# A tenth pair of up-projection tiles by half-size products in a fused decoder layer

## The chip, the cores and the metric

The kernel is one program on one core of a Trainium2 chip. The metric is device microseconds (us) of one execution. "The time before" is the median of three runs of the kernel as it stood.

## The reference, cut to what matters

One decoder layer, all in 32-bit floats, 512 tokens, model width 1024: a mixing sub-layer (not touched here) and then a gated MLP. `u` has 2 x 2816 columns: 22 column blocks of 128 in each of two halves, the half that goes through the silu and the half that it multiplies.

```python
h2 = rmsnorm(x, norm2_g[l]) * (1.0 + sc2) + sh2          # (512, 1024)
u = causal_dwconv(h2 @ w_up[l], conv_w[l], conv_b[l])    # w_up: (1024, 5632); conv over 3 tokens
a, v = jnp.split(u, 2, axis=-1)
x = x + gt2 * ((jax.nn.silu(a) * v) @ w_down[l])         # w_down: (2816, 1024)
```

## The kernel before

**Numbers in two parts.** TensorE takes its operands in a reduced format, so every operand is kept as a high part (a rounded copy, made on ScalarE) and a low part (what the rounding lost, made on VectorE as source minus high part). This pair of parts is called a form here. One product is three matmuls: high by high, low by high, high by low (`mm3`, L156 to L158). A second way to make a low part is used for some forms ("added"): ScalarE writes the negated source into the low part, GpSimd issues a DMA that adds the source to it, and the rounding of the format leaves the loss; VectorE then has nothing to do.

**The up-projection.** The result is made transposed, in 44 tiles of 128 columns of `u` by 512 tokens, each in a PSUM bank. Tile `2f` is block `f` of the silu half, tile `2f+1` the same block of the other half. A standard tile is 8 products (the 1024 inputs in eighths) of a 128x128 weight block with all 512 tokens, so 24 matmuls of 512 columns. Nine pairs of tiles (8 and 9, 12 and 13, ..., 40 and 41) are made together by seven half-size products in the manner of Strassen and Winograd, each of them 4 blocks by 256 tokens, so 12 matmuls of 256 columns: `P1` to `P7`. They need sums and differences of the quarters of the weights (`quads`: two tiles by two halves of the inputs), which VectorE makes in place in the loaded weights, and of the quarters of `h2` (`hB`, made into forms 1 to 4 of `h2`, `hS`, once for all pairs). The names in the order of steps:

- `n1` takes the loaded weights of the pair and makes weight form 1; `ns`, `nc`, `na`, `s4` make a sum of quarters (`e`) and three differences (in `raw`); `n5` is form 5; `f6 f2 f7 f3 f4` are the other five forms (tiles `wq`, 128x512).
- `P1` and `P5` come first, into bank `u` of the odd tile and into a spare bank `ux`. `S` is a ScalarE copy of the result of `P1` into the bank of the even tile; `P6` is then added to the result of `P1`, so `P6` waits for `S`. `w` is a ScalarE copy of `P5` to `w5u`. `V` and `W` (VectorE) add that copy to what `u` holds after `P6` and after `P7`, so `P7` waits for `V` and `P4` for `W`.
- `m0`, `m1` make the forms of the next two standard tiles (`whi`, `wlo`); `B0 B1 C0 C1` are the products of those tiles, in two pieces each, placed between the half-size products.
- `q6` or `p0` is the work on a finished tile 6 or 0 of a unit (`up_post`): ScalarE scales it with a tap of the convolution (L1646), VectorE adds the other two taps (L1647, L1648), ScalarE applies silu to an even tile (L1651), VectorE multiplies the pair (L1654). `x` takes one step from a list of further work on finished pairs (`gP`, `gQ`, `s`, `st`: operands for the down-projection), `g` and `G` steps of another gate, `t` steps that form the quarters of `h2`.

**What sets the order.** It is written by hand in two strings. `PRO` is played once: tiles 0 to 7 and the preparation of the first pair. `UNIT` is then played nine times, for pairs `j` = 2 to 10; in it a primed step belongs to the next pair. Every engine plays its instructions in the order of these strings, and waits by semaphores for what the others must have done. In the trace's times `PRO` covers tile 3 from 344.76 us, tile 4 from 350.23, tile 5 from 355.67, tiles 6 and 7 after it; the first `P1` of `UNIT` starts at 372.44. Loaded weights (`raw`) sit in three buffers that are filled from SyncE's queue as they come free.

Of the kernel before, what the change touches and what calls it, by code (L numbers as in the profile page):

```python
# [15 lines left out]
AF = mybir.ActivationFunctionType  # L16
ALU = mybir.AluOpType
# [7 lines left out]
KT = D // P  # L25
# [15 lines left out]
NB = 2  # L41
NU = 10
AWAY = (0, 1, 2, 3, 4, 5)
CUT = {"B": 6, "C": 7}
ADD = (1, 1)
PLAIN = ""
PRO = ("t t x M1 M2 t t t t F3 M3 F4 t A5 q0 G M4 q1 q2 F6 q3 M5 G M6 A7 x q4 x q5 G x t x n1' ns' f2' nc' n5' q6 na' s4' m0' x x M7 m1' g x f6' f7' x x x x f4'")
UNIT = ("P1 S P5 w n1' ns' x f3 B0 P6 P2 B1 V x f2' nc' n5' h1 x p-1 f4' P7 x m0' P3 h0' W K p2 g na' p0 C0 P4 x x x C1 s4' p1 x m1' x f6' x x x f7'")
PREP = ('sq2 sq3 rq2 rq3', '', 'nq0', 'fq0', 'nq1', '', 'lq0', 'fq1', 'nq2', '', 'lq1', 'fq2', 'nq3', 'lq2', 'fq3',
        'lq3', 'sk0 rk0 sk1 rk1', 'nk0 fk0 sk2 rk2', 'nk1 fk1 sk3 rk3', 'lk0 nk2 fk2', 'lk1 nk3 fk3 sa0 ra0',  # L50
# [61 lines left out]
def hybrid_layer_kernel(ctx: ExitStack, tc: tile.TileContext, d: dict, out: bass.AP, dbg=None):  # L112
    nc = tc.nc
    ve, sc, gp, pe, sp = nc.vector, nc.scalar, nc.gpsimd, nc.tensor, nc.sync
# [12 lines left out]
    def nm(s):  # L127
        uid[0] += 1
        return f"{s}_{uid[0]}"

    def G(shape, dt=F32, s="g"):
        return gran.tile([P] + list(shape), dt, tag="g", name=nm(s))

    def PS(s="ps"):
        return psum.tile([P, 512], F32, tag="b", name=nm(s))
# [12 lines left out]
    def f32(ap):  # L148
        return ap.bitcast(F32)

    def split(hi, lo, src, eng=None):
        sc.copy(hi, src)  # L152
        (eng or ve).tensor_tensor(lo, src, f32(hi), ALU.subtract)  # L153

    def mm3(o, ah, al, bh, bl, start, stop):
        pe.matmul(o, ah, bh, start=start, stop=False, skip_group_check=True)  # L156
        pe.matmul(o, ah, bl, start=False, stop=False, skip_group_check=True)  # L157
        pe.matmul(o, al, bh, start=False, stop=stop, skip_group_check=True)  # L158
# [56 lines left out]
    def issue():  # L215
        if len(issued) < len(loads):
            name, shape, pieces = loads[len(issued)]
            if name[0] == "d" and shape[0] * shape[1] <= 1024:
                raw = G(shape, s="rawd")
            else:  # L220
                raw = wp.tile([P] + shape, F32, tag="raw", name=nm("raw"), bufs=3)
            for sl, src in pieces:
                sp.dma_start(raw[sl], src)
            issued.append(raw)
# [3 lines left out]
    def take(name):  # L228

        i = taken[0]  # L230
        assert loads[i][0] == name, (loads[i][0], name)
        while len(issued) < min(i + (5 if loads[min(len(issued), len(loads) - 1)][0][0:2] in ("dx", "dy") else 3), len(loads)):
            issue()
        taken[0] += 1
        return issued[i]
# [55 lines left out]
    def next_parts(more=True, g=False, added=False):  # L291
        if not ahead:
            piece(g)
        w = ahead.pop(0)
        if more:
            piece(added=added)
        return w
# [1135 lines left out]
    def gate_step(n=2):  # L1433
        for _ in range(n):
            next(ada2, None)
# [105 lines left out]
    hB = {}  # L1541
# [83 lines left out]
    us = {}  # L1625
# [3 lines left out]
    def up_mm(st, sl, ks=range(KT)):  # L1629
        if st not in us:  # L1630
            us[st] = PS("u")
            if st not in wts:
                wts[st] = next_parts(st < nst - 2, added=False)
        hi, lo = wts[st]
        for k in ks:
            mm3(us[st][:, sl], hi[:, k], lo[:, k], h2T[k // 2][0][:, k % 2, sl], h2T[k // 2][1][:, k % 2, sl],
                k == 0 and not sl.start, k == KT - 1)
# [20 lines left out]
    quads = {}  # L1658
    forms7 = {}
    held = {}  # L1660
# [4 lines left out]

    def h2_form(o, q):
        hS[q] = hi, lo = [G([4, 256], F32R, s="hS") for _ in range(2)]
        split(hi, lo, hB.pop(o))

    tw = [(h2_sum, (0, 0), (0, 1), (0, 0)), (h2_sum, (0, 1), (1, 1), (0, 1)), (h2_sum, (1, 1), (1, 1), (0, 0)),  # L1670
          (h2_form, (0, 0), 1), (h2_sum, (1, 0), (1, 0), (1, 1)), (h2_form, (1, 1), 2), (h2_form, (0, 1), 3),
# [7 lines left out]
    def half_form(src):  # L1679
        t = G([2, 4, P], F32R, s="wq")  # L1680
        split(t[:, 0], t[:, 1], src)
        return t[:, 0], t[:, 1]

    def pair_open(j):
        raw = take(f"up{2 * j}")
        quads[j] = [raw[:, s, 4 * h:4 * h + 4] for s in range(2) for h in range(2)]
        t = wp.tile([P, 2, KT, P], F32R, tag="aw", name=nm("w3"), bufs=1)
        forms7[j] = {n: (t[:, 0, h:h + 4], t[:, 1, h:h + 4]) for n, h in ((1, 0), (5, 4))}
        split(*forms7[j][1], quads[j][0])
# [13 lines left out]
    def std_form(src, added):  # L1703
        hi = wp.tile(list(src.shape), F32R, tag="whi", name=nm("whi"))
        lo = wp.tile(list(src.shape), F32R, tag="wlo", name=nm("wlo"))
        if added:
            sc.activation(lo, src, AF.Copy, scale=-1.0)  # L1707
            gp.dma_start(f32(lo), src, accum_op=ALU.add)  # L1708
            return (hi, lo), lambda: sc.copy(hi, src)
        split(hi, lo, src)  # L1710
        return (hi, lo), None
# [13 lines left out]
    def std_make(j, s):  # L1725
        st = 4 * j + 2 + s
        if s == 0:
            raws[j] = take(f"up{2 * j + 1}")
        wts[st], high[st] = std_form(raws[j][:, s], ADD[s] and (s or j > NB))

# [5 lines left out]
        sc.copy(ws5[j], us["x", j][:, lo_half])  # L1736

    def banks(j):
        us[4 * j + 1] = PS("u")
        us["x", j] = PS("ux")  # L1740
        us[4 * j] = (held.pop if j == NU else held.get)(0)

    ws5 = {}

    def u_of(j, n, sl):
        return us[4 * j + n][:, sl]

    def do(j, tok):
        last = j == NU
# [8 lines left out]
    def do_(j, tok):  # L1758
        last = j == NU
        lo_, hi_ = lo_half, hi_half  # L1760
        w = forms7.get(j)
        u = partial(u_of, j)
        if tok == "P1":
            banks(j)
            sprod(u(1, lo_), w[1], h2_quarter(0, lo_), True)
            if last:
                pe.matmul(u(1, hi_), w[1][0][:, 0], h2_quarter(0, lo_)[0][0], start=False, stop=False,
                          skip_group_check=True)
        elif tok == "P5":
            sprod(us["x", j][:, lo_], w[5], h2_summed(1), True)  # L1770
        elif tok == "P6":
            sprod(u(1, lo_), w[6], h2_summed(2))
        elif tok == "P2":
            sprod(u(0, lo_), w[2], h2_quarter(1, lo_))
        elif tok == "P7":
            sprod(u(1, lo_), w[7], h2_summed(3))
        elif tok == "P3":
            sprod(u(0, hi_), w[3], h2_quarter(1, hi_))
        elif tok == "P4":
            sprod(u(1, lo_), w[4], h2_summed(4))  # L1780
        elif tok in ("B0", "B1", "C0", "C1"):
            up_mm(4 * j + (2 if tok[0] == "B" else 3), full, (range(0, CUT[tok[0]]), range(CUT[tok[0]], KT))[int(tok[1])])
        elif tok == "S":
            sc.copy(u(0, lo_), u(1, lo_))
        elif tok == "w":
            spare(j)
        elif tok == "V":
            ve.tensor_tensor(u(0, hi_), u(1, lo_), ws5[j], ALU.add)
        elif tok == "W":
            ve.tensor_tensor(u(1, hi_), u(1, lo_), ws5[j], ALU.add)  # L1790
        elif tok[0] == "p":
            up_post(4 * j + int(tok[1:]))
        elif tok == "x":
            step(1)
        elif tok in ("g", "G"):
            gate_step(2 if tok == "g" else 1)
        elif tok == "t":
            turn()
        elif tok[0] == "m":
            std_make(j, int(tok[1]))  # L1800
        elif tok[0] == "h":
            h = high.pop(4 * j + 2 + int(tok[1]))
            if h:
                h()
        elif tok == "K":
            park_late()
        elif tok == "n1":
            pair_open(j)
        elif tok == "ns":
            pair_sum(j)  # L1810
        elif tok == "nc":
            pair_less(j, 2, 0, 2)
        elif tok == "na":
            pair_less(j, 0, 4, 0)
        elif tok == "s4":
            pair_less(j, 1, 1, 0)
        elif tok == "n5":
            split(*w[5], quads[j][4])
        else:
            pair_form(j, int(tok[1]), {6: 0, 2: 1, 7: 2, 3: 1, 4: 3}[int(tok[1])])  # L1820
# [45 lines left out]
    def park_late():  # L1866
        if late26:
            j, st34 = late26.pop(0)
            sc.dma_start(pk34[:, j], f32(st34))
            gp.dma_start(pk26[:, AWAY.index(j)], f32(gQ.pop(j)))  # L1870
# [104 lines left out]
    lo_half, hi_half, full = slice(0, 256), slice(256, 512), slice(0, 512)  # L1975
# [27 lines left out]
    made[0] = 1  # L2003
    for tok in PRO.split():
        if tok[0] == "M":
            up_mm(int(tok[1]), full if tok[1] > "2" else hi_half)
            if tok == "M2":
                held[0] = us[0]
        elif tok[0] in "FA":
            piece(added=tok[0] == "A")  # L2010
            wts[int(tok[1])] = ahead.pop(0)
        elif tok[0] == "q":
            up_post(int(tok[1]))
        elif tok[0] in "txgG":
            do_(1, tok)
        else:
            do(NB - 1, tok)
# [71 lines left out]
    for q in range(NQ):  # L2089
        w = ready.pop(0)  # L2090
# [38 lines left out]
```

## Time and profile before

| | |
|---|---|
| median of 3 runs (671.79 to 672.07) | 671.82 us |
| the profiled execution: its time, and its span in the trace | 672.72 us, 670.9 us |
| PE (TensorE matmuls) busy | 663.2 us, 99% of the span |
| DVE (VectorE) busy | 582.8 us, 87% |
| ACT (ScalarE) busy | 400.5 us, 60% |
| POOL (GpSimd) busy | 74.1 us, 11% |

The profiled execution is 0.90 us above the median of the runs, 0.13%. Its span leaves out 1.8 us around the program. In a row of the trace's timeline stand: start, duration, engine, line, operation, tile written and tiles read, shape, and in brackets the idle time of the engine ahead of it and who ended that. Matmuls are pipelined: each starts before the one ahead has ended, so the pace is read from the starts.

### The profile page before, as it was taken

Reading aid. Unit: us, or ns where it says so; the run is one execution under the profiler, and the core shown is the slowest. Engines: PE = TensorE matmul, PEld = TensorE weight load, DVE = VectorE, ACT = ScalarE, POOL = GpSimd, SP = SyncE. Lnnn points to the kernel's source line nnn. Section 1 sums busy time; section 2 is a strip of 40 time slices with the busy share of each in tenths; the row PEclk is TensorE's granted clock in tenths of the full one; section 3 lists DMA queues with packets and bytes.
Section 4 is the critical chain, followed back from the end, with each engine's and each line's share of the span. In section 5 each row is a group of like instructions: output and inputs, shape, how many; then the busy total and the mean of one; then the engine's idle time right before and its main releaser. Section 6 shows DMA issues by size and latency. Waiting matters only on the chain.

```text
span 670.9 us, 11080 instructions
## 1 busy us (share of the span) xinstructions
PE 663.2 (99%) x4072; PEld 567.9 (85%) x4072; DVE 582.8 (87%) x1173; ACT 400.5 (60%) x775; POOL 74.1 (11%) x100
## 2 busy tenths in 40 slices
PE   8999999999999999999999999999999999999997
PEld 4677898788898889888998989999899998888886
DVE  4688988999998997789988999888988888988787
ACT  5565446766677688334665776577765775553431
POOL 1006144200100000211100111010110110000000
PEclk9999999999999999999999999999999999999999
DMA  9999443398042132537436488877889759999932
GB/s 278 286 321 271 149 157 130 100 293 264 26 149 95 33 103 96 195 103 220 153 95 157 103 228 240 239 214 211 228 236 250 224 153 345 366 343 398 380 111 95
DMA packets 111880, 134.84 MB, mean 201 GB/s; under 512 B 7322, under 2 KB 84946, under 8 KB 111826
## 3 DMA queue, kind: packets, MB, share of 16 engines
q1 hardware_dynamic: 102961, 106.89, 50.2%
q0 software_dynamic: 4720, 16.26, 10.7%
q10 hardware_dynamic: 4144, 10.99, 4.3%
q8 instruction: 32, 0.52, 0.3%
q14 instruction: 23, 0.18, 0.1%
HBM read 107.11 MB, written 16.00 MB: 183 GB/s over the span
## 4 chain that ended last, share of the span: by engine, by line
PE 91%; SPq 3%; DMA 2%; DVE 2%; issue 1%; ACT 0%; ACTq 0%; DVEq 0%
PE u L157 11%; PE u L156 11%; PE u L158 11%; PE dn L157 5%; PE dn L156 5%; PE dn L158 5%; PE pT L156 3%; PE pT L158 3%; PE pT L157 3%; PE F L1063 3%; PE oT L1091 3%; PE oh L158 2%; PE oh L156 2%; PE oh L157 2%; PE lev L1192 2%; SPq L321 2%
## 5 line engine op out<-in xcount | busy, mean ns | idle before, releaser
L156 PE MATMUL u<-h2h,whi 128*128 128x512 f32 (+1 forms) x200 | 75.1, 375 | 0.0
L157 PE MATMUL u<-h2l,whi 128*128 128x512 f32 (+1 forms) x200 | 74.9, 374 | 0.0
L158 PE MATMUL u<-h2h,wlo 128*128 128x512 f32 (+1 forms) x200 | 74.5, 373 | 0.0
L158 PEld LDWEIGHTS u<-h2h,wlo 128*128 128x128 f32 x200 | 37.7, 189 | 6.8
L1031 ACT ACTIVATE pt<-pt,mx 128x128 f32<-128x128 f32 (+3 forms) x64 | 35.8, 562 | 12.1 <-DVE mx L1015 11.1
L156 PEld LDWEIGHTS u<-h2h,whi 128*128 128x128 f32 x200 | 37.9, 189 | 5.5
L157 PEld LDWEIGHTS u<-h2l,whi 128*128 128x128 f32 x200 | 37.9, 189 | 5.2
L156 PE MATMUL pT<-hT,whi 128*128 128x512 f32 x96 | 39.2, 409 | 0.0
L153 DVE TENSOR_TENSOR wlo<-raw,whi 128x1024 fp32r<-128x1024 f32 (+1 forms) x31 | 36.0, 1161 | 3.6 <-ACT whi L152 3.4
L1651 ACT ACTIVATE y<-y 128x512 f32<-128x512 f32 x22 | 13.9, 633 | 41.7 <-DVE y L1648 41.6
L158 PE MATMUL pT<-hT,wlo 128*128 128x512 f32 x96 | 37.7, 393 | 0.0
L157 PE MATMUL pT<-hT,whi 128*128 128x512 f32 x96 | 37.6, 392 | 0.0
L152 ACT CAST whi<-raw 128x1024 fp32r<-128x1024 f32 (+1 forms) x31 | 30.9, 998 | 10.4 <-PE kva L158 4.4
L1647 DVE SCALAR_TENSOR_TENSOR y<-u,cv,y 128x511 f32<-128x511 f32 x44 | 32.8, 745 | 5.0 <-ACT y L1646 5.0
L1070 ACT COPY pT<-F 128x512 f32<-128x512 f32 (+2 forms) x52 | 25.8, 502 | 15.4 <-PE F L1063 11.2
L1015 DVE CUSTOM_DVE_ANT_0 pt<-S,cmask 128x128 f32<-128x128 f32 (+3 forms) x64 | 29.7, 485 | 5.7 <-PE S L1010 5.6
L1648 DVE SCALAR_TENSOR_TENSOR y<-u,cv,y 128x510 f32<-128x510 f32 x44 | 32.9, 749 | 1.5
L397 POOL TENSOR_TENSOR hrs<-hrs,mhalf 128x4 f32<-128x4 f32 (+2 forms) x16 | 20.9, 1314 | 120.7 <-DVE hrs L396 120.6
L1646 ACT ACTIVATE y<-u,cv 128x512 f32<-128x512 f32 x44 | 33.8, 770 | 0.0
L1708 POOL DMA_DIRECT2D wlo<-raw x17 | 14.6, 859 | 166.2 <-ACT wlo L1707 74.6
L153 DVE TENSOR_TENSOR wq<-raw,wq 128x512 fp32r<-128x512 f32 x45 | 30.7, 685 | 0.5 <-ACT wq L152 0.5
L158 PE MATMUL u<-hS,wq 128*128 128x256 f32 x108 | 30.6, 284 | 0.0
(471 smaller groups left out, 2175.3 us busy)
## 6 DMA issues: line engine op xcount, KB each, us to landing
raw<-in_w_up SPq DMA_DIRECT2D x44, 512.0 KB, 5.7
aw<-in_w_ada SPq DMA_DIRECT2D x24, 512.0 KB, 3.8
raw<-in_w_down SPq DMA_DIRECT2D x10, 1024.0 KB, 5.4
wlo<-raw POOLq DMA_DIRECT2D x19, 512.0 KB, 5.2
ada<-in_w_ada SPq DMA_DIRECT2D x32, 256.0 KB, 5.9
raw<-in_w_in SPq DMA_DIRECT2D x7, 1024.0 KB, 6.0
rawd<-in_w_down SPq DMA_DIRECT2D x12, 512.0 KB, 10.5
pk<-st ACTq DMA_DIRECT2D x11, 512.0 KB, 6.5
```

Of the source, the lines that this page charges most:

```text
L152: sc.copy(hi, src)
L153: (eng or ve).tensor_tensor(lo, src, f32(hi), ALU.subtract)
L156: pe.matmul(o, ah, bh, start=start, stop=False, skip_group_check=True)
L157: pe.matmul(o, ah, bl, start=False, stop=False, skip_group_check=True)
L158: pe.matmul(o, al, bh, start=False, stop=stop, skip_group_check=True)
L397: gp.tensor_tensor(o, o, mhalf[:, 0:n], ALU.pow)
L1015: ve.tensor_tensor_reduce(pt[:, sl], ps[:, sl], cmask[:, 512 - W:512], -1.0, 1e30, ALU.add, ALU.min, mx[:, e:e + 1])
L1031: sc.activation(pt[:, sl], pt[:, sl], AF.Exp, bias=mx[:, e:e + 1], scale=-1.0, accum_out=su[:, h % 2, e:e + 1])
L1070: sc.copy(pT, ps[:, 0:n * P])
L1646: sc.activation(y, u, AF.Identity, bias=cv[:, 132 + c:133 + c], scale=cv[:, 88 + c:89 + c])
L1647: ve.scalar_tensor_tensor(y[:, 1:], u[:, :T - 1], cv[:, 44 + c:45 + c], y[:, 1:], ALU.mult, ALU.add)
L1648: ve.scalar_tensor_tensor(y[:, 2:], u[:, :T - 2], cv[:, c:c + 1], y[:, 2:], ALU.mult, ALU.add)
```

## The change

Tiles 6 and 7 are no longer made by 48 matmuls of 512 columns at the end of `PRO`, but as a tenth pair by 84 matmuls of 256 columns (pair 1, `base(1)` = 6), which stand between tile 4 and the first `UNIT`, with tile 5 cut in two pieces (`Y0`, `Y1`) between them. The forms and differences of that pair are made in `PRO`. The low part of form 4 of `h2` is made the added way (`FADD`), in place of the low part of tile 7's weights; the weights of tile 6 and 7 are no longer made into standard forms.

```diff
+FADD = (4,)
-PRO = ("t t x M1 M2 t t t t F3 M3 F4 t A5 q0 G M4 q1 q2 F6 q3 M5 G M6 A7 x q4 x q5 G x t x n1' ns' f2' nc' n5' q6 na' s4' m0' x x M7 m1' g x f6' f7' x x x x f4'")
+PRO = ("t t x M1 M2 t t t t F3 M3 F4 t A5 q0 no G ns nc M4 n1 q1 n5 t na f6 x f2 P1 S P5 w q2 s4 G x P6 P2 Y0 V x f7 q3 x P7 f3 f4 n1' G q4 P3 W Y1 q6 ns' nc' P4 n5' m0' x f2' na' q5 f6' x s4' x m1' x g x f7' x x x f4'")
...
     def h2_form(o, q):
         hS[q] = hi, lo = [G([4, 256], F32R, s="hS") for _ in range(2)]
-        split(hi, lo, hB.pop(o))
+        src = hB.pop(o)
+        if q in FADD:
+            sc.activation(lo, src, AF.Copy, scale=-1.0)
+            gp.dma_start(f32(lo), src, accum_op=ALU.add)
+            sc.copy(hi, src)
+        else:
+            split(hi, lo, src)
...
+    def base(j):
+        return 4 * j if j >= NB else 4 * NB - 2
...
     def banks(j):
-        us[4 * j + 1] = PS("u")
+        us[base(j) + 1] = PS("u")
         us["x", j] = PS("ux")
-        us[4 * j] = (held.pop if j == NU else held.get)(0)
+        us[base(j)] = (held.pop if j == NU else held.get)(0)
...
+        elif tok[0] == "Y":
+            up_mm(5, full, (range(0, 5), range(5, KT))[int(tok[1])])
```

Where it moves instructions, three places. **ScalarE around the new pair's `w`.** Before, what follows tile 1's scaling (`y<-u_3919`, the row ahead of the first one shown) is tile 2's scaling and silu, and then the forms of tiles 6 and 7 from `raw_3853`:

```order
L1646 ACTIVATE y_4161<-u_3970,cv 128x512
L1651 ACTIVATE y_4161<-y_4161 128x512
L152 CAST w_795_4169<-raw_3853 128x1024
L1646 ACTIVATE y_4172<-u_4082,cv 128x512
L263 ACTIVATE wlo_4234<-raw_3853 128x1024
L265 CAST whi_4233<-raw_3853 128x1024
L152 CAST gP_4159<-y_4123 128x256
L1646 ACTIVATE y_4240<-u_4129,cv 128x512
```

Now `S` and `w` of the new pair stand there, then tile 2's scaling and silu, form 7 (`wq_4266`), tile 3's scaling, forms 3 and 4, the next pair's form 1 (`w_814`), tile 4's scaling (`u_4135`) and silu, and tile 6's scaling (`u_3894`, the held bank):

```order
L1798 COPY u_3894<-u_4186 128x256
L1750 COPY w5u_4213<-ux_4187 128x256
L1647 ACTIVATE y_4215<-u_3970,cv 128x512
L1652 ACTIVATE y_4215<-y_4215 128x512
L153 CAST wq_4266<-raw_3853 128x512
L1647 ACTIVATE y_4269<-u_4082,cv 128x512
L153 CAST wq_4290<-raw_3853 128x512
L153 CAST wq_4293<-raw_3853 128x512
L153 CAST w_814_4299<-raw_4107 128x512
L1431 COPY gt_3318<-ps_4221 128x512
L1647 ACTIVATE y_4303<-u_4135,cv 128x512
L1652 ACTIVATE y_4303<-y_4303 128x512
```

Tile 2's scaling moved behind a copy that needs the result of `P5`, and the work on tiles 3, 4 and 6 moved behind it.

**ScalarE ahead of the first `UNIT`'s `S`** (the copy of `u_4340` before, of `u_4399` now). Before, with tile 6's silu and the high part of the first standard tile (`whi`) at the head:

```order
L1651 ACTIVATE y_4274<-y_4274 128x512
L152 CAST whi_4284<-raw_4166 128x1024
L152 CAST gQ_4177<-y_4161 128x256
L1707 ACTIVATE wlo_4317<-raw_4166 128x1024
L152 CAST st_798_4178<-y_4161 128x256
L152 CAST wq_4325<-raw_4107 128x512
L152 CAST wq_4328<-raw_4107 128x512
L152 CAST gP_4159<-s_792_4160 128x256
L152 CAST gQ_4177<-s_792_4160 128x256
L152 CAST st_799_4179<-s_792_4160 128x512
L152 CAST wq_4337<-raw_4107 128x512
L1784 COPY u_3894<-u_4340 128x256
```

Now, from tile 5's scaling on (ahead of these rows stand tile 6's silu, `w_814<-e` for form 5, `whi_4355` and form 2, `wq_4360`):

```order
L1647 ACTIVATE y_4364<-u_4249,cv 128x512
L153 CAST wq_4371<-raw_4107 128x512
L153 CAST gQ_4274<-y_4215 128x256
L1721 ACTIVATE wlo_4379<-raw_4128 128x1024
L153 CAST st_809_4275<-y_4215 128x256
L153 CAST gP_4168<-s_795_4169 128x256
L153 CAST wq_4389<-raw_4107 128x512
L153 CAST gQ_4274<-s_795_4169 128x256
L153 CAST st_810_4276<-s_795_4169 128x512
L153 CAST wq_4396<-raw_4107 128x512
L1798 COPY u_3894<-u_4399 128x256
```

The nine instructions right ahead of `S` are the same as before in number and kinds; form 6 (`wq_4371`) is now the first of them, and form 5, form 2 and tile 5's scaling came in between tile 6's silu and them.

**VectorE in the same place.** Before, with the low parts of form 5 (`w_812<-e`), tile 6's two taps, two differences, and the low part of the first standard tile:

```order
L153 TENSOR_TENSOR w_812_4263<-e_4266,w_812_4263 128x512
L1647 SCALAR_TENSOR_TENSOR y_4274<-u_4208,cv,y_4274 128x511
L1648 SCALAR_TENSOR_TENSOR y_4274<-u_4208,cv,y_4274 128x510
L1698 TENSOR_TENSOR raw_4107<-e_4266,raw_4107 128x512
L1698 TENSOR_TENSOR raw_4107<-raw_4107 128x512
L153 TENSOR_TENSOR wlo_4285<-raw_4166,whi_4284 128x1024
```

Now, from tile 6's taps on:

```order
L1648 SCALAR_TENSOR_TENSOR y_4330<-u_3894,cv,y_4330 128x511
L1649 SCALAR_TENSOR_TENSOR y_4330<-u_3894,cv,y_4330 128x510
L1707 TENSOR_TENSOR e_4335<-raw_4107 128x512
L1712 TENSOR_TENSOR raw_4107<-raw_4107 128x512
L154 TENSOR_TENSOR w_814_4299<-e_4335,w_814_4299 128x512
L154 TENSOR_TENSOR wlo_4356<-raw_4128,whi_4355 128x1024
L1851 TENSOR_TENSOR s_795_4169<-s_795_4169,y_4123 128x256
L154 TENSOR_TENSOR wq_4360<-raw_4107,wq_4360 128x512
L1712 TENSOR_TENSOR raw_4107<-e_4335,raw_4107 128x512
L1648 SCALAR_TENSOR_TENSOR y_4364<-u_4249,cv,y_4364 128x511
L1649 SCALAR_TENSOR_TENSOR y_4364<-u_4249,cv,y_4364 128x510
L1655 TENSOR_TENSOR y_4303<-y_4303,y_4364 128x512
```

The next pair's sum `e` and its form 5 moved behind tile 6's taps, and the difference that form 6 is made of (`raw<-e,raw`) behind the low part of a standard tile.

More of the change, by code (lines that the diff above doesn't have):

```diff
@@ L1682, in half_form, with pair_take @@
         return t[:, 0], t[:, 1]
+    def base(j):
+        return 4 * j if j >= NB else 4 * NB - 2
+    def pair_take(j):
+        raw = take(f"up{base(j) // 2}")
+        quads[j] = [raw[:, s, 4 * h:4 * h + 4] for s in range(2) for h in range(2)]
     def pair_open(j):
-        raw = take(f"up{2 * j}")
-        quads[j] = [raw[:, s, 4 * h:4 * h + 4] for s in range(2) for h in range(2)]
+        if j not in quads:
+            pair_take(j)
         t = wp.tile([P, 2, KT, P], F32R, tag="aw", name=nm("w3"), bufs=1)
@@ L1738, in banks @@
     def banks(j):
-        us[4 * j + 1] = PS("u")
+        us[base(j) + 1] = PS("u")
         us["x", j] = PS("ux")
-        us[4 * j] = (held.pop if j == NU else held.get)(0)
+        us[base(j)] = (held.pop if j == NU else held.get)(0)
     ws5 = {}
     def u_of(j, n, sl):
-        return us[4 * j + n][:, sl]
+        return us[base(j) + n][:, sl]
     def do(j, tok):
@@ L1806, in do_ @@
             park_late()
+        elif tok == "no":
+            pair_take(j)
         elif tok == "n1":
```

## The prediction

> **What bounds the kernel now.** I read the page first, then the busy time by stretch, then the timeline of each engine around `PRO`.
>
> ```profile
> span 670.9 us, 11080 instructions
> PE 663.2 (99%) x4072; PEld 567.9 (85%) x4072; DVE 582.8 (87%) x1173; ACT 400.5 (60%) x775; POOL 74.1 (11%) x100
> PEclk9999999999999999999999999999999999999999
> wlo<-raw POOLq DMA_DIRECT2D x19, 512.0 KB, 5.2
> ...
> 355.67:379.42 23.75, 23.75 (x118) 20.16 (x116) 20.40 (x33) 17.18 (x30) 2.80 (x4) 1.00 0.50 117
> ```
>
> PE is busy for 99% of the span at the full granted clock. The last line is one stretch, from tile 5's first matmul to the first `P6` of `UNIT`: its length, then busy time of PE, weight loads, DVE, ACT and POOL. PE is never idle in those 23.75 us, but DVE is busy for 20.40 of them: 3.35 us are free. So each PE instruction saved is time saved, as long as DVE and ACT keep ahead, and they have little room.
>
> The pace of PE is in the starts:
>
> ```profile
> 350.23 0.39 PE L156 MATMUL u<-h2h,whi 128*128 128x512 f32 x1
> 355.67 0.39 PE L156 MATMUL u<-h2h,whi 128*128 128x512 f32 x1
> 372.44 0.28 PE L156 MATMUL u<-h2h,w 128*128 128x256 f32 x1
> 375.31 0.40 PE L156 MATMUL u<-h2h,whi 128*128 128x512 f32 x1
> 379.42 0.28 PE L156 MATMUL u<-hS,wq 128*128 128x256 f32 x1
> 382.17 0.28 PE L158 MATMUL u<-h2h,wq 128*128 128x256 f32 x1
> ```
>
> They are the first matmuls of tiles 4 and 5 (24 matmuls apart: 5.44/24 = 0.2267 us for 512 columns), of the first `UNIT`'s `P1` and of `B0` (24 apart: 2.87/24 = 0.1196 for 256 columns), and the first of `P6` and last of `P2`. `B0` takes 379.42 - 375.31 = 4.11.
>
> **The change part by part. PE's own work.** Removed: 48 x 0.2267 = 10.88. Added: 84 x 0.1196 = 10.05. If PE never waits the change is worth -0.83 us: 671.0, which is 0.12% and inside the 0.2% that a measurement of this kernel can tell from no change. That is the most it can bring.
>
> Here a page of the Trainium skill would have it otherwise. TensorE: Matmul & The Clock Gate, section "Wait — 56ns, not 53.3ns?", puts the start-to-start time of a warm matmul at its columns over 2.4 GHz plus about 2.5 ns, which as an estimate gives 109.2 ns for 256 and 215.8 for 512 columns, and a saving of 1.19 us. The trace agrees on the slope (226.7 - 119.6 = 107.1 ns for 256 columns) but its fixed part is about 13 ns for each matmul, so the row decides; by the page the total below would be 0.36 us lower.
>
> **DVE's and ACT's work.** The durations, from one piece of each queue:
>
> ```profile
> 369.74 0.77 ACT L1646 ACTIVATE y<-u,cv 128x512 f32<-128x512 f32 x1
> 372.52 0.63 ACT L1651 ACTIVATE y<-y 128x512 f32<-128x512 f32 x1 [2.01 <-DVE y L1648]
> 373.06 1.03 ACT L152 CAST whi<-raw 128x1024 fp32r<-128x1024 f32 x1
> 374.00 0.40 ACT L152 CAST gQ<-y 128x256 fp32r<-128x256 f32 x1
> 374.30 1.06 ACT L1707 ACTIVATE wlo<-raw 128x1024 fp32r<-128x1024 f32 x1
> 375.26 0.39 ACT L152 CAST st<-y 128x256 fp32r<-128x256 f32 x1
> 375.56 1.14 ACT L152 CAST wq<-raw 128x512 fp32r<-128x512 f32 x2
> 376.60 0.40 ACT L152 CAST gP<-s 128x256 fp32r<-128x256 f32 x1
> 376.91 0.40 ACT L152 CAST gQ<-s 128x256 fp32r<-128x256 f32 x1
> 377.21 0.62 ACT L152 CAST st<-s 128x512 fp32r<-128x512 f32 x1
> 377.73 0.62 ACT L152 CAST wq<-raw 128x512 fp32r<-128x512 f32 x1
> 378.25 0.36 ACT L1784 COPY u<-u 128x256 f32<-128x256 f32 x1
> 378.56 0.36 ACT L1736 COPY w5u<-ux 128x256 f32<-128x256 f32 x1
> ...
> 370.90 0.74 DVE L1647 SCALAR_TENSOR_TENSOR y<-u,cv,y 128x511 f32<-128x511 f32 x1
> 371.68 0.75 DVE L1648 SCALAR_TENSOR_TENSOR y<-u,cv,y 128x510 f32<-128x510 f32 x1
> 372.35 0.68 DVE L1698 TENSOR_TENSOR raw<-e,raw 128x512 f32<-128x512 f32 x1
> 373.06 0.69 DVE L1698 TENSOR_TENSOR raw<-raw 128x512 f32<-128x512 f32 x1
> 374.13 1.23 DVE L153 TENSOR_TENSOR wlo<-raw,whi 128x1024 fp32r<-128x1024 f32 x1 [0.37 <-ACT whi L152]
> 375.27 0.42 DVE L1835 TENSOR_TENSOR s<-y,s 128x256 f32<-128x256 f32 x1
> 375.60 0.42 DVE L153 TENSOR_TENSOR gQ<-y,gQ 128x256 fp32r<-128x256 f32 x1
> 382.49 0.43 DVE L1788 TENSOR_TENSOR u<-u,w5u 128x256 f32<-128x256 f32 x1 [1.12 <-PE u L158]
> ```
>
> Start to start, an ACT instruction takes its duration less 0.09 (0.53 for 512 elements, 0.95 for 1024, 0.30 for 256, 0.67 for a scaling), a DVE one its duration less 0.08 (0.60, 1.14, 0.33; 0.78 for a tap with its dependent successor). ACT's silu starts 0.09 after DVE's last tap ends (372.43 to 372.52); DVE starts 0.04 after ACT (374.09 to 374.13) and after PE (382.17 + 0.28 to 382.49).
>
> DVE gains a sum and three differences, seven low parts (11 x 0.60) and `V` and `W` (2 x 0.33): +7.3; it loses two low parts of 1.14 (tile 6's weights and form 4 of `h2`): net +5.0, against the 3.35 that are free in the stretch and what is free while tile 4 runs. ACT gains seven high parts, `S`, `w` and a negated copy of `h2` (3.7 + 0.6 + 0.95) and loses three of 1024 elements (2.85): +2.4. POOL keeps the same number of DMAs: the one for tile 7's low part (512 KB) goes, one of 512 KB for form 4 comes; it is issued near 354 behind form 5's high part and by the 5.2 us of its row lands near 359, where `P4` needs it after 370: nothing. On SP's queue nothing is added; the buffer of the new pair's weights comes free with its form 4's low part, near 367 in the walk below, and what is then loaded is read first after `S`, at 382: nothing.
>
> **The walk** (PE's position by its pace, the others by the rows above, in the order the change shows). `P1` starts at 355.67 in tile 5's place; its forms are made while tile 4 runs. `P5` ends at 355.67 + 24 x 0.1196 + 0.16 = 358.71. Then:
> - ACT: `w` 358.75, tile 2's scaling 359.0 to 359.8. DVE: its taps 359.83 and 360.61, to 361.36. ACT: silu 361.45, form 7's high part 361.99, tile 3's scaling 362.5, forms 3, 4 and 1, the gate's copy, and tile 4's scaling from 365.3 to 366.1. DVE: form 7's low part 362.65, tile 3's taps 363.33 and 364.11, the product 364.9, `s` 365.6, low parts of form 3 at 365.95, of form 4 at 366.55, of the next pair's form 1 at 367.15; tile 4's taps at 367.75 and 368.5, to 369.28.
> - PE meanwhile: the gate's two matmuls 0.45, `P6 P2` 2.87, `Y0` 3.40, `P7 P3` 2.87, `Y1` 2.04, `P4` 1.44: the next pair's `P1` starts at 371.6 and ends at 373.1. `P6` (forms ready 357.3, needed 359.0), `P7` (363.3, 365.3) and `P3` (366.6, 366.7) do not wait, `P3` barely.
> - ACT, idle since 366.1: tile 4's silu 369.37, tile 6's scaling 369.91. DVE: its taps 370.72 and 371.50, to 372.25, the sum `e` 372.17 to 372.85. ACT: tile 6's silu 372.34, form 5's high part 372.88 to 373.50. DVE: its low part to 374.23.
> - So `P5` of the first `UNIT`, due at 373.1, starts at 373.53, and its third matmul, the first that reads the low part, waits again until 374.3. **First loss: about 1.0 us.** `P5` ends at 375.5, `B0` at 379.6.
> - ACT: `whi` 373.4, form 2 374.4, tile 5's scaling 374.9 to 375.7. Form 6's high part needs the difference `raw<-e,raw`, which stands on DVE behind `wlo` (374.5, after `whi`), `s` (375.64) and form 2 (375.97): it runs 376.57 to 377.25. Form 6 starts at 377.34, and from the first of the same nine instructions to `S` it is 378.25 - 374.00 = 4.25 in the rows: `S` starts at 381.6 and ends at 381.95.
> - `P6` waits for `S`: from 379.6 to 382.0. **Second loss: 2.4 us.** In the trace of before `S` ended at 378.61, 0.81 ahead of `P6`.
>
> So the first `UNIT`'s `P6` starts at 382.0 instead of 379.42, 2.57 later: -0.83 + 1.0 + 2.4. `V` follows on DVE near 385.85, behind six more low parts, when `P6`, `P2` and `B1` are done at about 386.2: a further 0.1 for `P7`.
>
> **What is late next.** In the second `UNIT` `S` hangs on loads. The rows: PE's next `P6`; DVE's low part that frees the buffer; SP's load and the ACT instruction that waits for its landing, in the first and in the slowest unit; and the `S` that followed in the latter.
>
> ```profile
> 400.44 0.28 PE L156 MATMUL u<-hS,wq 128*128 128x256 f32 x1
> 401.42 0.68 DVE L153 TENSOR_TENSOR wq<-raw,wq 128x512 fp32r<-128x512 f32 x1
> 402.13 0.99 SPq L223 DMA_DIRECT2D raw<-in_w_up  x2
> 406.58 1.06 ACT L1707 ACTIVATE wlo<-raw 128x1024 fp32r<-128x1024 f32 x1 [2.29 <-DMA raw<-in_w_up]
> 423.16 1.77 SPq L223 DMA_DIRECT2D raw<-in_w_up  x2
> 428.21 1.06 ACT L1707 ACTIVATE wlo<-raw 128x1024 fp32r<-128x1024 f32 x1 [2.89 <-DMA raw<-in_w_up]
> 440.43 0.37 ACT L1784 COPY u<-u 128x256 f32<-128x256 f32 x1
> ```
>
> A load is issued 0.03 after the freeing low part and read 4.45 to 5.05 later; `S` comes 440.43 - 428.21 = 12.22 after that. The freeing low part now ends near 385.95, so the second `S` ends at 385.98 + (4.45 to 5.05) + 12.22 + 0.36 = 403.0 to 403.6; `P6` is due at 382.0 + 21.02 (400.44 - 379.42) + 0.1 = 403.1. A loss of 0 to 0.5; I take 0.2, nearer the lower landing. After that DVE's wait for `P6` (1.12 in the row of `V`) is room that grows back. The down-projection is untouched.
>
> Sum: -0.83 + 1.0 + 2.4 + 0.1 + 0.2 = +2.9. The walk is made on the profiled execution, 672.72, so 675.6 on that scale; on the median of the runs it is 671.82 + 2.9 = 674.7, the number I give.
>
> **The rivals.**
> 1. *PE keeps its lead (not slower).* The mechanism: `S` runs before PE needs it. It decides at `S`'s end: 379.55 or earlier, 2.4 us earlier than walked. For it: before, `S` was 0.81 early, and the same nine instructions stand ahead of it; against it: both silu waits of the walk (tiles 4 and 6) are chains of dependent steps, which free time elsewhere doesn't shorten. 671.82 - 0.83 = 671.0.
> 2. *Only one of the two waits comes.* If tile 4's taps run earlier than walked, by the 3.3 us that ACT idles for them, form 5 is in time and `S` too by half: 671.82 - 0.83 + 1.0 = 672.0 to 673.
> 3. *The units never catch up.* The loop of freeing low part, landing and `S` with a landing of 5.05 is as long as a unit; then the second loss of 0.5 and about 0.1 in each of seven units come on top: 674.7 + 0.3 + 0.7 to 1 = 676.
> 4. *The clock drops behind the wait.* After a wait of 2.4 us PE could run slower; if `P6` and `P2` behind it took twice their 2.87, that is 677.6. The granted clock is full in all 40 slices, and no wait of PE in this stage can show what one does. The Trainium skill's page TensorE: Matmul & The Clock Gate, Part 1, has such a rule, and halves the clock only after an idle window of about 3.4 us, longer than the wait forecast; no run here shows it.
>
> **How the numbers follow.** The forecast has 0.68 (own range 673.9 to 675.5: its losses of 1.0 and 2.4 each within a few tenths), rival 1 0.14, rival 2 0.08, rival 3 0.08, rival 4 0.02. From 672.0 to 676.2 the range holds the forecast and rivals 2 and 3, 0.84. Slower by over 0.2% (above 673.16): the forecast, rivals 3 and 4, and a quarter of rival 2, 0.80. Within: rival 1 and most of rival 2, 0.17, a few hundredths going to faster for what neither row nor walk holds.
>
> **What would show it.** In the profile of the changed kernel: 84 half-size matmuls at 0.12 start to start and none of tiles 6 and 7 at 512; a wait of PE for ACT's and DVE's form 5 (`w`) of about 0.5 each, and one of about 2.4 for ACT at the first `P6` of `UNIT`, with `S` (the line of the copy to `u`) near 381.6; later units without waits of PE. If PE shows no wait there the prediction is wrong and rival 1 holds; if waits come back in each unit, rival 3.

## The result and the profile after

The changed kernel took 676.2 us (median; 675.35 to 677.02), the kernel before 671.95 beside it (671.79 to 672.85): ratio 1.006 (95% interval 1.0043 to 1.0078). The forecast was 674.7 in a range of 672.0 to 676.2: slower, as predicted, and at the very end of the range. A second set of executions gave a little less (below). Two executions far outside all others are in the median of their set, but in no ratio and no count: one of the last set of the reordered kernel below (938.06 us at a mean clock of 0.656) and one of the kernel before beside it (1337.41 us at 1.000).

The page of the changed kernel, one execution of 675.35 us at the full clock:

```profile
span 673.6 us, 11173 instructions
PE 663.6 (99%) x4108; PEld 568.4 (84%) x4108; DVE 588.4 (87%) x1184; ACT 402.9 (60%) x782; POOL 74.1 (11%) x100
PE   8999999999999999999999899999999999999998
PEclk9999999999999999999999999999999999999999
```

The span is 2.7 us longer. DVE has 5.6 us more work and ACT 2.4 more; the walk had 5.0 and 2.4. PE's row has a new 8 in the 23rd slice, about 370 to 387 us, the end of `PRO` and the start of the first `UNIT`. The waits of PE between 330 and 570 us, where the kernel before has none (engine, what it works on, its line, what it waited for: us, times, longest):

```profile
PE u L157 <- ACT u L1798: 2.1, 1, 2.1
PE ux L157 <- ACT w L153: 0.3, 1, 0.3
PE ux L159 <- DVE w L154: 0.2, 1, 0.2
PE u L159 <- DMA wlo<-raw: 0.2, 1, 0.2
```

The first is `P6` of the first `UNIT`, which waits for `S` (L1798 is the copy to `u`); the next two are `P5`, which waits for form 5's high and low part; the last is a standard tile of the second `UNIT` that waits for the landing of its added low part. The same places in the timeline of PE, start by start, with the first matmul of `P1` in tile 5's place and the first of the second `UNIT`'s `P6` at the two ends:

```profile
355.42 0.28 PE L157 MATMUL u<-h2h,w 128*128 128x256 f32 x1
...
372.74 0.28 PE L159 MATMUL u<-h2h,w 128*128 128x256 f32 x1
373.30 0.39 PE L157 MATMUL ux<-hS,w 128*128 128x256 f32 x1 [0.28 <-ACT w L153]
373.52 0.28 PE L158 MATMUL ux<-hS,w 128*128 128x256 f32 x1
374.02 0.39 PE L159 MATMUL ux<-hS,w 128*128 128x256 f32 x1 [0.22 <-DVE w L154]
...
381.70 0.39 PE L157 MATMUL u<-hS,wq 128*128 128x256 f32 x1 [2.11 <-ACT u L1798]
381.93 0.28 PE L158 MATMUL u<-hS,wq 128*128 128x256 f32 x1
...
384.68 0.40 PE L157 MATMUL u<-h2h,whi 128*128 128x512 f32 x1
...
399.04 0.40 PE L158 MATMUL u<-h2l,whi 128*128 128x512 f32 x1
399.62 0.50 PE L159 MATMUL u<-h2h,wlo 128*128 128x512 f32 x1 [0.18 <-DMA wlo<-raw]
399.96 0.40 PE L157 MATMUL u<-h2h,whi 128*128 128x512 f32 x1
...
403.37 0.28 PE L157 MATMUL u<-hS,wq 128*128 128x256 f32 x1
```

What counts is the distance between starts beyond PE's pace: 0.56 - 0.12 = 0.44 and 0.50 - 0.12 = 0.38 at `P5`, 2.27 at `P6` in the same reckoning, and 0.58 - 0.23 = 0.35 at the landing. The bracket gives about 0.16 less each time. The matmul behind each wait is late by another 0.1 (381.93 comes 0.23 behind 381.70 where the pace is 0.12), so the losses are 1.03 at `P5`, 2.38 at `P6` and 0.47 at the landing. Behind the first matmul of `P7` stands 0.09 too, without a wait in the list.

And why `S` is late, in ACT's timeline:

```profile
369.12 0.63 ACT L1652 ACTIVATE y<-y 128x512 f32<-128x512 f32 x1 [3.38 <-DVE y L1649]
372.09 0.63 ACT L1652 ACTIVATE y<-y 128x512 f32<-128x512 f32 x1 [1.66 <-DVE y L1649]
372.63 0.62 ACT L153 CAST w<-e 128x512 fp32r<-128x512 f32 x1
377.03 0.62 ACT L153 CAST wq<-raw 128x512 fp32r<-128x512 f32 x1 [1.63 <-DVE raw L1712]
381.29 0.37 ACT L1798 COPY u<-u 128x256 f32<-128x256 f32 x1
```

In these rows ACT waits three times for DVE, 6.7 us in all, each time with later work queued behind a silu or a form that isn't ready: the silus of tiles 4 and 6, then form 6. Form 5 (`w<-e`) stands right behind tile 6's silu, though it needs nothing of it. Its sum `e` was no earlier: on DVE it stands behind tile 6's taps and ends at 372.59, so both queues held form 5.

```profile
371.91 0.68 DVE L1707 TENSOR_TENSOR e<-raw 128x512 f32<-128x512 f32 x1
```

### The profile page after: what moved, and what is told of

Its sections match the earlier page's. It is cut to its first block, busy times and chain, and to the rows that moved or that the text cites. A ratio compares the mean times of both kernels' runs of the same rounds, so it can differ in the third digit from the quotient of the medians.

```text
span 673.6 us, 11173 instructions
## 1 busy us (share of the span) xinstructions
PE 663.6 (99%) x4108; PEld 568.4 (84%) x4108; DVE 588.4 (87%) x1184; ACT 402.9 (60%) x782; POOL 74.1 (11%) x100
## 4 chain that ended last, share of the span: by engine, by line
PE 85%; DVE 6%; DMA 3%; SPq 3%; issue 1%; ACT 1%; ACTq 0%; DVEq 0%
PE u L159 9%; PE u L158 9%; PE u L157 9%; PE dn L158 5%; PE dn L157 5%; PE dn L159 5%; PE pT L157 3%; PE pT L159 3%; PE pT L158 3%; PE F L1064 3%; PE oT L1092 3%; PE oh L159 2%; PE oh L158 2%; PE oh L157 2%; SPq L322 2%; PE lev L1193 2%
## 5 line engine op out<-in xcount | busy, mean ns | idle before, releaser
L157 PE MATMUL u<-h2h,whi 128*128 128x512 f32 (+1 forms) x192 | 71.9, 374 | 0.0
L158 PE MATMUL u<-h2l,whi 128*128 128x512 f32 (+1 forms) x192 | 71.7, 374 | 0.0
L159 PE MATMUL u<-h2h,wlo 128*128 128x512 f32 (+1 forms) x192 | 71.4, 372 | 0.2 <-DMA wlo<-raw 0.2
L159 PEld LDWEIGHTS u<-h2h,wlo 128*128 128x128 f32 x192 | 36.2, 188 | 7.1 <-DMA wlo<-raw 0.6
L157 PEld LDWEIGHTS u<-h2h,whi 128*128 128x128 f32 x192 | 36.3, 189 | 5.1
L158 PEld LDWEIGHTS u<-h2l,whi 128*128 128x128 f32 x192 | 36.3, 189 | 4.9
L157 PE MATMUL u<-hS,wq 128*128 128x256 f32 x120 | 34.0, 283 | 2.1 <-ACT u L1798 2.1
L154 DVE TENSOR_TENSOR wq<-raw,wq 128x512 fp32r<-128x512 f32 x50 | 34.2, 685 | 1.1 <-ACT wq L153 1.1
L153 ACT CAST wq<-raw 128x512 fp32r<-128x512 f32 x50 | 30.8, 618 | 6.3 <-DVE raw L1712 2.8
```

## The experiments

Three readings stood against each other. *Order*: the loss comes from which step is queued behind which on ACT and DVE. *Amount*: 5 us more on DVE and 2.4 on ACT don't fit this stretch, in whatever order. *Clock*: on top of the waits, PE runs slower behind them.

**The changed kernel again.** No edit.

> The changed kernel once more, unchanged, for more executions with their granted clocks. Theory 1 (PE's waits in the profile, 0.28 + 0.22 + 2.11 + 0.18 us, cost more than their length, because the clock of PE drops behind the long wait in some executions): most executions show a mean granted clock of 0.997 and lie at 676 to 677, those at 1.000 lie at 675.0 to 675.5; 0.3% of 675 us at half clock is one stretch of about 4 us. Rival (the clock has nothing to do with it, the time scatters with the landings of the loads): times at 0.997 and 1.000 don't differ.

675.67 us (675.55 to 676.39) against 672.36: ratio 1.0053 (1.0041 to 1.0065). Only one of the five executions was at 0.997, where most were expected, and one at the full clock took as long (676.39 against 676.30), so this set alone does not settle the clock by its times. The profile does. Here the profiled execution caught what the first had not. Busy time by stretch of this execution (length; PE, weight loads, DVE, ACT, POOL; granted clock; DMA share and GB/s), and then the same stretch of the execution shown above:

```profile
382.00:386.00 4.00, 4.00 (x24) 4.00 (x24) 3.60 (x7) 2.73 (x6) 0.00 (x0) 0.60 0.53 131
386.00:390.00 4.00, 4.00 (x30) 3.74 (x29) 3.65 (x8) 2.19 (x4) 0.00 (x0) 1.00 0.82 227
```

```profile
382.00:386.00 4.00, 4.00 (x30) 3.63 (x28) 4.00 (x9) 2.73 (x6) 0.00 (x0) 1.00 0.54 132
```

The granted clock is 0.60 right behind the wait, and 24 matmuls run where 30 did. PE's timeline in the execution with the drop:

```profile
381.65 0.49 PE L157 MATMUL u<-hS,wq 128*128 128x256 f32 x1 [2.11 <-ACT u L1798]
...
382.15 0.41 PE L159 MATMUL u<-hS,wq 128*128 128x256 f32 x1
382.37 0.41 PE L157 MATMUL u<-hS,wq 128*128 128x256 f32 x1
...
385.14 0.31 PE L158 MATMUL u<-h2l,wq 128*128 128x256 f32 x1
385.28 0.28 PE L159 MATMUL u<-h2h,wq 128*128 128x256 f32 x1
385.40 0.28 PE L157 MATMUL u<-h2h,wq 128*128 128x256 f32 x1
...
386.11 0.40 PE L157 MATMUL u<-h2h,whi 128*128 128x512 f32 x1
```

The pace is 0.213 us instead of 0.12 from 381.65 to 385.14, 3.5 us. Where the other execution started `B1` at 384.68 after a `P6` at 381.70, this one started it at 386.11 after 381.65: 1.48 us lost. The later loss at the landing (0.47) is not there in this execution, so about 1.0 stays; the spans differ by 0.9.

**The wait filled with matmuls.** 17 half-size products that nothing reads, written to a bank that the unit fills afterwards:

```diff
+            if j == NB and tok == "P6":
+                us[4 * j + 3] = PS("u")
+                for _ in range(FILL):          # FILL = 17
+                    pe.matmul(us[4 * j + 3][:, lo_half], h2T[0][0][:, 0, 0:P],
+                              h2T[0][0][:, 0, lo_half], start=True, stop=True, skip_group_check=True)
```

> The changed kernel, and in the long wait ahead of the first unit's P6 17 matmuls of 256 columns of h2 by h2, written to the bank that the fourth tile of that unit starts afresh later; their result is used nowhere. PE works in the 2.1 us in which it waited. Theory 1 (clock drops behind the wait): granted clock 1.000 in every execution, time 674.4 to 675.2, that is 0.8 to 1.8 below the changed kernel although PE does more. Rival: the same 676.2 and the same clocks as the changed kernel, or later, since 2.0 us of matmuls were added.

675.2 us (674.77 to 675.59), ratio 1.0042 (1.003 to 1.0054): 0.5 us below the changed kernel on the same chip, where 0.8 to 1.8 was expected against its first set. That is not the clock's: the changed kernel's median there is of an execution at the full clock. Nor is it shown to come from the 17 matmuls: in its profiled execution this kernel was ahead by 0.5 already at `P5` (372.80 against 373.30), and from there to `P6` both take 8.40.

```profile
378.93 2.19 PE L2043 MATMUL u<-h2h 128*128 128x256 f32 x17
381.20 0.39 PE L158 MATMUL u<-hS,wq 128*128 128x256 f32 x1
```

PE is busy up to 0.08 us ahead of `P6` and `P6` runs at full pace; the clock is 0.999 or 1.000 in all five executions. The wait for `S` itself is only hidden, not shortened, so the loss stays. That no execution had the half-clock stretch points to PE's idling as what brings it, and not the work that follows; with a drop in 4 of the changed kernel's 9 executions, five without one would come by chance about once in 19 times.

**`P1` and `S` of the next pair ahead of the first `UNIT`.**

```diff
-... P4 n5' m0' x f2' na' ...
+... P4 n5' P1' S' m0' x f2' na' ...
+            if j == NB and tok in ('P1', 'S'):
+                continue
```

> The first unit's P1 and S alone are moved in the order: right behind form 5 of that pair, ahead of the 13 other ACT instructions. PE's order stays. Theory 2 (S's place in ACT's queue is what costs 2.1 to 2.4): P6 waits 0.4 at most, for its low part, and the time falls by about 2, to 674. Theory 3 (VectorE is behind with its work, and S only shows it first): the wait comes back at P7, about 2.2 us for V, which stands on VectorE behind the low parts; time within 0.5 of the changed kernel, 676.

675.97 us (674.96 to 677.59), ratio 1.0053: no better. `S` is now done early and the wait at `P6` is gone. It came back one step later, at `P7`, which waits for `V`:

```profile
386.48 0.36 PE L158 MATMUL u<-hS,wq 128*128 128x256 f32 x1 [2.04 <-DVE u L1803]
```

```profile
386.00:390.00 4.00, 3.52 (x18) 3.55 (x19) 3.96 (x8) 2.17 (x4) 0.00 (x0) 0.62 0.69 192
```

The half-clock stretch moved with it. So the late `S` was a symptom: everything on ACT and DVE at this place is late by as much.

**Less work on DVE.** The low parts of five forms of the new pair are not made, and the high part is read in their place, so tiles 6 and 7 of this kernel don't hold the reference's values; it is there for its time alone. DVE loses five of the seven added low parts, 3 us:

```diff
     def pair_form(j, n, src):
+        if j < NB:
+            t = G([2, 4, P], F32R, s="wq")
+            sc.copy(t[:, 0], quads[j][src])
+            forms7[j][n] = t[:, 0], t[:, 0]
+            return
```

> The five 128x512 low parts of the new pair's forms 2, 3, 4, 6 and 7 are not made (their high part is read in their place, so tiles 6 and 7 are not the reference's): 3.0 us less work on VectorE in PRO, all orders and PE's matmuls as in the changed kernel. Theory 3 (VectorE's backlog alone): both waits go, the time is near 671.82 - 0.83 = 671.0. Theory 2 (the order: what stands ahead of S on ACT, with form 6 behind VectorE's difference): the wait for form 5 (1.0) goes, the one of P6 for S stays near 2.3, time 674.6 to 675.2.

675.37 us (673.94 to 675.52), ratio 1.0042. `P5` no longer waits. `P6` does:

```profile
380.76 0.38 PE L157 MATMUL u<-hS,wq 128*128 128x256 f32 x1 [1.93 <-ACT u L1803]
```

3 us less on DVE brought `P6` 0.94 us forward (1.20 counted from `P1` in tile 5's place, which started 0.26 later here), and `S` still hangs on the same chain: DVE's difference, form 6, and the instructions behind it on ACT. Taking away 3 of the 5 us took away `P5`'s loss and little of `P6`'s: against *amount*, though not yet decisive.

**The order changed, and one low part moved off DVE.** The same products and forms. Forms stand ahead of the scaling and silu of a tile that they don't need, `w` comes behind tile 2's work, the next pair's sum (`ns'`) ahead of `q6`, and the first standard tile's low part is made by ACT and the adding DMA (`m0'`, its high part apart as `h0'`). The first `UNIT` (steps with @) has an order of its own; the later ones keep theirs.

```diff
-PRO = ("... n1 q1 n5 t na f6 x f2 P1 S P5 w q2 s4 G x P6 P2 Y0 V x f7 q3 x P7 f3 f4 n1' G q4 P3 W Y1 q6 ns' nc' P4 n5' m0' x f2' na' q5 f6' x s4' x m1' ...
+PRO = ("... n1 q1 na n5 f7 t f6 x f2 P1 f4 S P5 q2 s4 x x P6 P2 G Y0 f3 w V q3 P7 n1' m0' f2' x G q4 P3 W Y1 ns' q6 nc' x na' P4 n5' q5 h0' m1' f6' x x s4' ... @P1 @S g @P5 @w @n1' @ns' @x @B0 @h1 @f3 @P6 f7' @P2 @B1 @V ...
-        wts[st], high[st] = std_form(raws[j][:, s], ADD[s] and (s or j > NB))
+        wts[st], high[st] = std_form(raws[j][:, s], ADD[s])
```

> The changed kernel with the same products and forms, in another order in PRO and in the first UNIT: forms stand ahead of the scaling and silu of a tile that they don't need, w of the new pair comes behind tile 2's work, the next pair's sum and form 5 come earlier, and the first standard tile of the second pair has its low part made as the other tiles' is (ACT and the adding DMA, 1.14 us of VectorE fewer). Theory of the order (the loss is that forms, silus and steps queue behind each other; nothing is wrong with half-size products as such): walked through with the rows' durations, PE then waits nowhere, P5, P6 and P7 of the first UNIT included, and what is left is PE's own saving of 0.83 us: 671.2 to 671.8 us where the kernel before stands at 672.0 to 672.4, and the granted clock stays at 1.00 in every execution. Theory of the amount (5 us more on VectorE and 2.4 on ACT can't be hidden in this stretch whatever their order): waits of at least 1 us in all come back somewhere between 357 and 405 us, and the time is 673.5 or more. Between the two: waits of some tenths at the adding DMA's landing near 399 us, which the walk has at its edge, 672.0 to 672.5.

671.56 us (670.96 to 672.63, 11 executions) against 672.25: ratio 0.9985 (0.9976 to 0.9993). In a second set, beside the kernel with the order alone:

> e5_best once more, on the same chip as e9_order_only: 0.5 to 1 us below the kernel before, no wait of PE between 330 and 570 us, clock 1.00 throughout.

671.59 against 672.47: ratio 0.9985 (0.9976 to 0.9994). Both times PE waits nowhere in the stretch, and the time is 0.7 to 0.9 us below the kernel before. From the first `P1` (tile 5 before) to the first `P6` of `UNIT` PE takes 22.99 us in both profiled executions, where the kernel before takes 23.75: -0.76, PE's own work. Page and ACT's timeline:

```profile
span 669.3 us, 11174 instructions
PE 663.1 (99%) x4108; PEld 568.7 (85%) x4108; DVE 586.4 (88%) x1183; ACT 404.0 (60%) x783; POOL 75.2 (11%) x101
...
367.05 0.64 ACT L1652 ACTIVATE y<-y 128x512 f32<-128x512 f32 x1 [2.22 <-DVE y L1649]
370.19 0.63 ACT L1652 ACTIVATE y<-y 128x512 f32<-128x512 f32 x1 [1.66 <-DVE y L1649]
370.73 0.60 ACT L153 CAST w<-e 128x512 fp32r<-128x512 f32 x1
373.82 0.60 ACT L153 CAST wq<-raw 128x512 fp32r<-128x512 f32 x1
376.59 0.37 ACT L1798 COPY u<-u 128x256 f32<-128x256 f32 x1
```

Form 5 is made 1.9 us earlier than in the changed kernel, form 6 no longer waits, and `S` runs 4.7 us earlier, at 376.59, where `P6` starts at 378.04. (0.4 of each is an earlier start of the whole stretch in this execution.)

**The order alone.** As before, but that low part is made by DVE again, so that every engine has the changed kernel's work.

```diff
-... n1' m0' f2' x G q4 ... na' P4 n5' q5 h0' m1' f6' ...
+... n1' f2' x G q4 ... na' P4 n5' m0' q5 m1' f6' ...
-        wts[st], high[st] = std_form(raws[j][:, s], ADD[s])
+        wts[st], high[st] = std_form(raws[j][:, s], ADD[s] and (s or j > NB))
```

> The order of e5_best alone: the second pair's first standard tile has its low part made by VectorE again, as in the changed kernel, so that VectorE has exactly the changed kernel's work; only the order of PRO and of the first UNIT differs from it. Theory of the order: walked through with the rows' durations, PE waits 0.3 us at P6 and 0.2 at P7 of the first UNIT and nowhere else: 0.4 us more than e5_best, 671.5 to 672.3 us, 4 us less than the changed kernel with the same amount of work on every engine. Theory of the amount, which after e5_best could still say that the 1.14 us taken off VectorE did it: 674 us or more.

671.89 us (671.34 to 672.55, 11 executions), ratio 0.9993 (0.9984 to 1.0002); 0.3 above the kernel with both edits, run beside it: PE loses 0.12 us at `P6` and 0.18 at `P7` by its starts, and nothing else in the stretch. This decides between *order* and *amount*. The stretch from 355 to 382 us, of the kernel with the order alone, and then of the changed kernel:

```profile
355.00:382.00 27.00, 27.00 (x182) 24.75 (x181) 25.63 (x46) 19.21 (x37) 2.95 (x5) 1.00 0.55 137
```

```profile
355.00:382.00 27.00, 24.38 (x157) 21.75 (x156) 23.04 (x40) 16.90 (x33) 1.92 (x3) 1.00 0.41 100
```

DVE can be busy 25.63 of 27 us here. In the changed kernel it was busy for 23.04 and stood idle for 4, nearly all of it (3.7) waiting for ACT, which was waiting for DVE; with the new order it waits 1.1 for ACT. The silus of tiles 2, 4 and 6 wait 6.7 us for DVE in this window in both kernels. What is gone is ACT's wait for the differences that its forms are made of (2.8 in the changed kernel, none here), and what PE needs next no longer stands behind a silu. The work fitted; its order did not.

**One low part moved off DVE, the changed kernel's order.**

```diff
-... f3 f4 n1' G q4 P3 W Y1 q6 ns' nc' P4 n5' m0' x f2' ...
+... f3 f4 n1' G m0' q4 P3 W Y1 q6 ns' nc' P4 n5' h0' x f2' ...
-        wts[st], high[st] = std_form(raws[j][:, s], ADD[s] and (s or j > NB))
+        wts[st], high[st] = std_form(raws[j][:, s], ADD[s])
```

> The changed kernel with one step changed: the low part of the second pair's first standard tile is made as the other standard tiles' is (negated copy on ACT, adding DMA), started behind the next pair's form 1 where ACT is idle, so that 1.14 us of VectorE's work (wlo, which stood between form 5's and form 2's low parts) leaves the queue ahead of form 6 and S. Theory of the order: form 5's two waits stay (0.3 to 0.5 each), P6's wait goes from 2.2 to about 1.4 us, and in all PE loses 0.9 us less: 674.3 to 674.9 us at the full clock. If the clock drops only behind a wait of about 2 us, the half-clock stretch (about 1.5 us) is gone here in all executions and the mean is lower still than the changed kernel's by 1 to 1.7 us; if the drop follows any wait, some executions stay near 676. Theory of the amount: VectorE's load falls by 1.14 of 5.0 us, so the loss falls by about a quarter, 0.8 us: no different in size, but then form 5's waits would shrink too.

674.82 us (673.87 to 675.13, 8 executions), ratio 1.0032 (1.0022 to 1.0042): 1.4 below the changed kernel's first set and 0.85 below its second (1.7 and 0.7 when each is taken against the kernel before beside it).

```profile
PE u L157 <- ACT u L1798: 1.2, 1, 1.2
PE u L159 <- DMA wlo<-raw: 0.3, 1, 0.3
PE ux L157 <- ACT w L153: 0.3, 1, 0.3
PE ux L159 <- DVE w L154: 0.2, 1, 0.2
```

`P5`'s waits stay and `P6`'s is 0.9 shorter, as *order* had it. And the clock was 0.999 or 1.000 in all eight executions: a wait of 1.2 did not bring the half-clock stretch.

**Form 4's low part back on DVE** (`FADD = ()` instead of `(4,)`).

> The changed kernel with form 4 of h2 made by VectorE's difference again (FADD empty): ACT has one negated copy of 1024 elements fewer, VectorE one low part of 1.14 us more, and one DMA goes. Walked through, it lies where VectorE was waiting for tile 4's matmuls anyway: no difference from the changed kernel, 675.3 to 676.4 us, the same waits at form 5 and P6. Were VectorE's amount of work the cause, it would be 1.1 us slower than the changed kernel, 676.8 to 677.5.

676.33 us (676.12 to 676.57), ratio 1.0055 (1.004 to 1.0071): the changed kernel's loss, with one more low part of 1024 elements on DVE and the same four waits of PE, the one for the landing longer (0.6 against 0.2). No cost or gain of that part shows in the time.

**Form 5 ahead of tile 6.**

```diff
-... W Y1 q6 ns' nc' P4 n5' m0' ...
+... W Y1 ns' nc' n5' q6 P4 m0' ...
```

> The changed kernel with the next pair's sum, second difference and form 5 ahead of tile 6's scaling, taps and silu (q6) instead of behind them. Theory of the order: form 5's two waits go (0.3 to 0.5 each), but tile 6's silu, and with it the first standard tile's high and low part and form 6, come later by as much: PE waits at B0 instead (about 0.4 for ACT's high part and 0.8 for VectorE's low part) and at P6 about 2.5 us for S: the time is no better, 675.3 to 676.4 us, or 0.3 above the changed kernel. If form 5's place by itself were the first loss, 674.8 or less.

676.19 us (675.87 to 677.63), ratio 1.0056 (1.0042 to 1.007).

```profile
PE u L157 <- ACT u L1798: 2.3, 1, 2.3
PE u L159 <- DVE wlo L154: 0.5, 1, 0.5
PE u L159 <- DMA wlo<-raw: 0.5, 1, 0.5
```

`P5`'s waits are gone, and the same half microsecond stands at `B0`'s low part. One step moved alone hands the lateness on; the whole stretch had to be put in order.

## Why the prediction was right, and what it missed

- **PE's own work, -0.83**: held, at -0.76 by the starts. The half-size products run at 0.12 start to start, and the kernel in which PE doesn't wait is 0.69 and 0.88 us below the kernel before in its two sets.
- **First loss, about 1.0 at `P5`**: 1.03, for the reason given: form 5 behind tile 6's silu on ACT, and its sum behind tile 6's taps on DVE.
- **Second loss, 2.4 at `P6`**: 2.38; `S` started at 381.29 where the walk had 381.6. The whole stretch ran 0.3 earlier than walked, since `P1` in tile 5's place started at 355.42 instead of 355.67.
- **0.1 at `P7`**: 0.09.
- **0.2 in the second `UNIT`**: 0.47 was lost there, but not at `S`. It was the added low part of a standard tile, whose DMA landed after its matmul was due; the walk had looked at the loads only. That this term came near is luck: its place was wrong.
- Sum: -0.76 + 1.03 + 2.38 + 0.09 + 0.47 = 3.2, where the walk had 2.9. It agrees with the trace: from `P1` in tile 5's place to the second `UNIT`'s `P6` the changed kernel takes 403.37 - 355.42 = 47.95 us, and the kernel before, from tile 5 on, 400.44 - 355.67 = 44.77. The spans differ by 2.7 only, because the profiled execution of before lost 0.5 to the changed kernel's elsewhere, half of it ahead of tile 5 and half behind the second `UNIT`'s `P6`. The changed kernel's executions at the full clock lie 3.3 to 3.4 above the medians of before. So for an execution at the full clock the working holds.
- **Rival 4, the clock**: this is the term that was missed. It got 0.02, and beside it stood the page of the Trainium skill, TensorE: Matmul & The Clock Gate, Part 1, which halves the clock only after an idle window of about 3.4 us. Here a wait of 2.1, with two of 0.3 and 0.2 some 8 us ahead of it, was enough in 4 of 9 executions, and waits of 1.9 to 2.3 in 14 of 28 over five kernels. The size was wrong too: priced at 2.87 on the ground that `P6` and `P2` take twice as long, it measured 1.48 behind the wait, since only 3.5 us ran at the slower pace, and less in the end. Over both sets of the changed kernel the four executions with the drop have a median of 676.46, the five at the full clock 675.61: 0.85 apart. The first set, with three of four, lies 4.25 above its kernel before; the second, with one of five, 3.31.
- **The range**: the first set's median stands at its very end, and that it is not outside is luck. The sum of 2.9 holds nothing for the clock; how many of four executions have the drop decides it.
- **Rivals 1 and 2** fell with `P5`'s and `P6`'s waits, **rival 3** with the later units, which have no wait but the landing's.
- One sentence of the prediction pointed the wrong way though its walk did not: that DVE gains 5.0 us "against the 3.35 that are free in the stretch", and what is free while tile 4 runs. With the same 5 us in another order PE lost 0.3.

## What to carry to other kernels

When a step is moved to an engine with little free time, don't compare sums: write out both queues step by step and look for what stands behind an instruction that waits, here a form behind a silu it had nothing to do with, and its sum behind that tile's taps. A late step that is moved alone passes its lateness to the next; count a queue as mended only when nothing behind it is late. And price a wait of TensorE of two microseconds at more than its length: here about half the executions with one lost some 0.9 us more.

## What the runs showed of the hardware

In three profiled executions TensorE ran slower for one stretch of 3.2 to 3.5 us behind a single wait of 1.9 to 2.1 us, with a pace of 0.213 instead of 0.120 us for a product of 256 columns (a granted clock of 0.60 and 0.62 in the windows of 4 us shown). By the mean clock of the execution, 0.996 or 0.997, it happened in 14 of the 28 executions of the five programs whose profile has a wait of 1.9 to 2.3 us there; three more profiles, with waits of 2.1, 2.1 and 2.3, are of executions without it. In the 45 executions of the programs whose longest wait in this stretch was 1.2 or less, or was filled with matmuls, the mean clock was 0.999 or 1.000 each time. The slower stretch need not begin where the wait ends. In the execution of the kernel with less work on DVE it began 0.7 us into the work behind it, 2.6 us after the wait began (`P6` starts at 380.76):

```profile
381.34 0.31 PE L158 MATMUL u<-hS,wq 128*128 128x256 f32 x1
381.45 0.40 PE L159 MATMUL u<-hS,wq 128*128 128x256 f32 x1
381.65 0.42 PE L157 MATMUL u<-hS,wq 128*128 128x256 f32 x1
```

What decides when it begins, why only half of the executions have it, and where between 1.2 and 1.9 us the point lies, no run shows.
